# Attention scores of both maps from three products, the low part of the queries over 64 rows, in a two-layer hybrid mixer

## The chip, the cores and the metric

The kernel runs on one core of a Trainium2 chip. The metric is the device time of one execution in microseconds (us), the median of several runs. A page of one profiled execution and its trace were read as well.

## The reference, cut to what matters

Two layers are computed on 1024 latent tokens and 256 context tokens of width 1024. Only the attention matters here: 4 heads, two maps per head (m = 0, 1), 64 wide, over 1280 keys for a latent query.

```python
q_lat = apply_rope(rms_norm(split_heads_qk(q), qk_norm_g[0]), rope_cos, rope_sin)
k_lat = apply_rope(rms_norm(split_heads_qk(k), qk_norm_g[1]), rope_cos, rope_sin)
def diff_attend(q, k, v, lam):
    s = jnp.einsum('bhmqd,bhmkd->bhmqk', q, k).astype(jnp.float32) * (QK_DIM ** -0.5)
    p = jax.nn.softmax(s, axis=-1)
    p = p[:, :, 0] - lam * p[:, :, 1]
    return jnp.einsum('bhqk,bhkd->bhqd', p.astype(v.dtype), v)
```

## The kernel before, in words

The order of the work is written out by hand: every engine runs its instructions in the order in which the Python code calls them. PE is TensorE, DVE is VectorE, ACT is ScalarE, POOL is GpSimd and SP issues most DMAs.

Each layer first makes the gates, the Fourier and pooling parts and a first share of the output projection. Then come the projections of keys, queries and values (line 360, two token tiles of 128 per "post"), and then the attention. In a post of keys or queries (`qk_post`) DVE applies the rotary tables; for the keys the factor of the norm is multiplied on one post later (`k_late`), and for the queries it is kept aside in `rq` and enters only at the exponential. The unscaled queries are stored to memory (`qd`) and read back per tile.

For precision, each query and key is split into a high and a low part. The keys stand transposed in `kT`, one tensor per head and map, with the high part in rows 0 to 63 and the low part in rows 64 to 127. The query stands as [high, low] and [low, high], so that two matmuls over 128 rows give all four products.

The attention goes over units: one token tile of 128 queries and one head, 4 units to a tile, and in layer 0 two more units for the two context tiles. `step(i)` puts parts of four units side by side:

- unit i: the scores of map 0 and, later in the step, those of map 1 (line 915, six matmuls each), the row maxima (line 925) and their product with the norm factor (line 928) on DVE, the exponentials on ACT (line 943)
- unit i-1: `combine` joins the two maps (lines 952 to 969, DVE and POOL)
- unit i-2: `p_trans` transposes the probabilities in pieces of 4, 4 and 2 blocks (line 982, copied out by line 985 on DVE for the first piece and line 987 on ACT for the others), and `pv` multiplies with the values (line 998, copied out by line 1001 on ACT)
- unit i+1: `q_trans` transposes the split queries (line 894, copied out by line 901 on ACT); unit i+2: `q_split` on DVE

When a tile's four units are done, `z_trans` transposes its result (line 1031), ACT copies the high part out (line 1034) and DVE makes the low part (`z_low`, line 1039). In the same step follows the first half of the tile's output projection and in the next step the second half (line 1061, twelve matmuls each). `PIECES` and `ENDS` name these steps.

PSUM has 8 banks: two score tiles of three banks (`PS`), and two banks for everything else (`PX`). A matmul that starts a score tile waits until the exponential that read the same tile before is done.

On ACT, `pv`'s copy (line 1001) stands between the exponentials of the two maps:

```python
            if old:
                pv(old)
            if cur:
                expo(cur, 1)
```

Of the kernel before, what the change touches and what calls it, by code (L numbers as in the profile page):

```python
# [31 lines left out]
def build(tc, I, out):  # L32
# [52 lines left out]
    # silu(c) = 0.5 c (1 + tanh(c/2))  # L85
# [44 lines left out]
    def mod_finish(l, k, sh, scl):  # L130
        """sh, scl: [128, n, 2] products for the n channel tiles from k on"""
# [11 lines left out]
    def mod0_load(q):  # L143
        """shift and scale for the channel tiles 2q and 2q + 1"""
# [46 lines left out]
    def mod_acc(src, c0, sides, res, eng2=None):  # L191
        """elementwise over k: acc[p, s, col] = sum_k w[k*128+p, col] * silu(c)_s[k*128+p] for 512 columns"""
# [66 lines left out]
    def x_rms(x, r):  # L259
        """r = 1 / rms of the rows of x"""  # L260
# [90 lines left out]
    def proj_tok(H, W, npair, post):  # L351
        """token-major [128 tokens, 256 columns], two token tiles to a bank"""
# [42 lines left out]
    def fourier_fft(A, ntok):  # L395
        """8-point transform over the high digit of the token; 2-point for the context"""
# [90 lines left out]
    def pooling(l, ct, wpb, gs, b, ntok):  # L487
        psc = pscT[:, l, ct:ct + 1]
        zs = []
        for c0, L in ((0, SEQ), (SEQ, CTX)):  # L490
# [17 lines left out]
            else:  # L508
                # windows of 8 replace those of 2, and of 16 those of 4
# [22 lines left out]
    def layer(l, src, dst, carry):  # L532
# [19 lines left out]
        # ---- tokens, and with them the fourier gate  # L552
# [106 lines left out]
        # small tables for what follows  # L659
# [58 lines left out]
        # ---- rest of the output projection, its loads ahead of the stores of the gates  # L718
# [45 lines left out]
        # ---- k, q, v  # L764
# [69 lines left out]
        for c in range(2):  # L834
            W = w_get()
            proj_tok(H, W, npA, qk_post(0, c))
# [520 lines left out]
```

## Time and profile before

| | |
|---|---|
| median of 3 runs | 1475.15 us (1474.24 to 1475.6) |
| span of the profiled execution | 1476.5 us, the only time given for it, 1.35 us above the median |
| busy: PE, DVE, POOL, ACT | 1391.2, 992.0, 774.4, 579.9 us |
| attention, layer 0 and layer 1 | about 505 to 815 us and 1199 to 1476 us of the span |
| matmuls of the scores, line 915 | 768 with 184.4 us busy, besides those of the context tiles |
| row maxima, line 925; the products behind them, line 928 | 132 each; 194.9 us and 85.0 us busy |

Busy time counts the whole of each instruction, and matmuls overlap, so a busy PE need not be the limit. What a stage is worth is read from the wait that ends last in it.

### The profile page before, as it was taken

To read this page: it belongs to the slowest core of one execution; us is meant where nothing else is said; L and a number is where in the kernel's file an instruction comes from. 1 tells how busy PE (TensorE), PEld (TensorE's weight loads), DVE (VectorE), ACT (ScalarE), POOL (GpSimd) and SP (SyncE) were. 2 spreads that over 40 slices of the span, in tenths; PEclk is the share of its full clock that TensorE was granted. 3 is DMA by queue.
4 is the path that set the end of the run, shared out by engine and by line. 5 is a ranking of instruction groups with operands and counts; after the bars stand their busy time and mean duration, and the time that the engine had idled before them with its cause. 6 is when DMAs were issued, how large, how long until landed. Compare 5 with 4: busy or idle time off the path is not lost.

```text
span 1476.5 us, 24260 instructions
## 1 busy us (share of the span) xinstructions
PE 1391.2 (94%) x9364; PEld 1245.2 (84%) x9364; DVE 992.0 (67%) x1667; ACT 579.9 (39%) x1230; POOL 774.4 (52%) x827
## 2 busy tenths in 40 slices
PE   7899999899999988899998999999999998999998
PEld 1678899789999977888887788888999997888887
DVE  2854458876883298788988653482564249888995
ACT  2633112101323274666665342120232236565663
POOL 2543122557783066666667742245986027666663
PEclk9999999999999999999999999999999999999999
DMA  9221332673232121112113222527212111111210
GB/s 353 96 85 33 127 112 90 223 247 126 72 115 72 57 73 58 58 46 70 44 66 107 83 64 81 177 82 243 99 55 93 45 44 44 43 44 44 77 39 30
DMA packets 65155, 137.09 MB, mean 93 GB/s; under 512 B 7312, under 2 KB 19728, under 8 KB 65040
## 3 DMA queue, kind: packets, MB, share of 16 engines
q1 hardware_dynamic: 49712, 108.82, 22.1%
q10 hardware_dynamic: 15328, 26.72, 5.3%
q8 instruction: 74, 1.21, 0.4%
q14 instruction: 41, 0.34, 0.1%
HBM read 105.63 MB, written 29.88 MB: 92 GB/s over the span
## 4 chain that ended last, share of the span: by engine, by line
PE 48%; DVE 22%; issue 4%; POOL 3%; DMA 3%; ACT 2%; ACTq 0%; POOLq 0%; DVEq 0%; SPq 0%
PE x L360 18%; DVE sm L925 7%; PE x L1061 6%; PE S L915 6%; PE x L340 5%; PE x L998 5%; DVE sm L928 3%; PE x L753 3%; PE x L982 2%; DVE t L985 1%; DVE qs L882 1%; DMA xpart<-e 1%; DVE t L210 1%; PE x L894 1%; PE x L856 1%
## 5 line engine op out<-in xcount | busy, mean ns | idle before, releaser
L360 PE MATMUL x<-wh,t 128*128 128x256 f32 x2432 | 445.0, 284 | 0.0
L360 PEld LDWEIGHTS x<-wh,t 128*128 128x128 f32 x2432 | 380.7, 192 | 1.8 <-issue 1.0
L360 PE MATMUL x<-wl,t 128*128 128x256 f32 x1216 | 344.3, 283 | 1.4 <-DVE wl L318 0.9
L925 DVE TENSOR_REDUCE sm<-S 128x1 f32<-128x1280 f32 (+1 forms) x132 | 194.9, 1477 | 73.6 <-PE S L915 72.6
L360 PEld LDWEIGHTS x<-wl,t 128*128 128x128 f32 x1216 | 233.0, 192 | 3.1 <-issue 1.2
L943 ACT ACTIVATE t<-S,sm,rq 128x1280 f32<-128x1280 f32 (+1 forms) x140 | 184.5, 1321 | 24.4 <-DVE sm L928 23.4
L915 PE MATMUL S<-t,e 128*128 128x512 f32 (+1 forms) x768 | 184.4, 376 | 3.0 <-ACT e L901 1.5
L340 PE MATMUL x<-t,wh 128*128 128x512 f32 (+1 forms) x640 | 172.0, 379 | 10.1 <-DVE t L289 5.1
L998 PE MATMUL x<-t,t 128*128 128x128 f32 x1312 | 159.1, 277 | 2.3 <-DVE t L985 1.7
L998 PEld LDWEIGHTS x<-t,t 128*128 128x128 f32 x1312 | 155.6, 194 | 5.5 <-DVE t L985 2.0
L915 PEld LDWEIGHTS S<-t,e 128*128 128x128 f32 x768 | 128.7, 193 | 21.9 <-ACT t L943 2.8
L340 PEld LDWEIGHTS x<-t,wh 128*128 128x128 f32 x640 | 113.2, 190 | 33.1 <-DVE t L289 5.9
L318 POOL TENSOR_TENSOR wl<-st,wh 128x1024 fp32r<-128x1024 f32 x36 | 92.7, 2576 | 86.3 <-ACT wh L317 85.7
L317 ACT ACTIVATE wh<-st 128x1024 fp32r<-128x1024 f32 x64 | 64.8, 1058 | 138.8 <-DMA xpart<-e 45.0
L966 POOL TENSOR_TENSOR t<-t,t 128x768 f32<-128x768 f32 (+1 forms) x64 | 116.1, 1813 | 5.3
L958 POOL TENSOR_SCALAR t<-t,sm 128x768 f32<-128x768 f32 x62 | 85.6, 1381 | 51.9 <-DVE sm L954 33.2
L982 PE MATMUL x<-ident,t 128*128 128x128 f32 x636 | 102.6, 277 | 6.0 <-DVE e L1064 4.9
L1061 PE MATMUL x<-wh,e 128*128 128x512 f32 (+1 forms) x312 | 100.3, 389 | 3.9 <-ACT t L987 2.7
L753 PE MATMUL x<-wh,t 128*128 128x512 f32 x288 | 93.5, 403 | 8.9 <-DVE t L528 4.7
L340 PE MATMUL x<-t,wl 128*128 128x512 f32 (+1 forms) x320 | 99.5, 372 | 0.0
L210 DVE SCALAR_TENSOR_TENSOR t<-t,sc,t 128x512 f32<-128x512 f32 x98 | 92.2, 982 | 2.2 <-DMA t<-in_wmB_dram 1.8
L982 PEld LDWEIGHTS x<-ident,t 128*128 128x128 f32 x636 | 75.1, 142 | 17.1 <-DVE e L1064 7.5
(225 smaller groups left out, 2324.6 us busy)
## 6 DMA issues: line engine op xcount, KB each, us to landing
st<-in_w_in_dram SPq DMA_DIRECT2D x48, 512.0 KB, 4.2
t<-in_wmB_dram ACTq DMA_DIRECT2D x24, 512.0 KB, 5.4
xpart<-e ACTq DMA_DIRECT2D x36, 256.0 KB, 4.4
t<-xpart SPq DMA_DIRECT2D x18, 512.0 KB, 3.9
t<-in_wmS_dram SPq DMA_DIRECT2D x16, 512.0 KB, 9.4
st<-in_w_out_dram SPq DMA_DIRECT2D x16, 512.0 KB, 4.7
t<-in_x_dram SPq DMA_DIRECT2D x10, 512.0 KB, 10.3
e<-in_x_dram SPq DMA_DIRECT2D x20, 256.0 KB, 4.8
```

The lines of the kernel that those rows point to most:

```text
L210: dve.scalar_tensor_tensor(a, w, sk, a, MULT, ADD)
L318: lo_eng[hf].tensor_tensor(lo[:, sl, :], st, hi[:, sl, :].bitcast(F32), SUB)
L340: pe.matmul(p[:, :m], lhsT=W[wi][:, k, ct * 128:ct * 128 + 128], rhs=H[k][hi][:, c0:c0 + m], start=(n == 0), stop=(n == 3 * KT - 1))
L360: pe.matmul(bank[:, i * 256:i * 256 + 256], lhsT=H[k][hi][:, j * 128:j * 128 + 128], rhs=W[wi][:, k, :], start=(n == 0), stop=(n == 3 * KT ...
L753: pe.matmul(ps, lhsT=zr[k][zi][:, j * 128:j * 128 + 128], rhs=W[wi][:, k, :], start=(n == 0), stop=(n == 11))
L915: pe.matmul(S[:, i * nk + c:i * nk + c + n], lhsT=s["qT"][i][:, m * 2 + f, :], rhs=kT[2 * h + m][:, k0 + c:k0 + c + n], start=(f == 0), st ...
L925: dve.tensor_reduce(mx, S[:, :nh * nk].rearrange("p (h k) -> p h k", h=nh), AX.X, ALU.max)
L943: act.activation(p[:, sl], S[:, sl], AF.Exp, bias=nb[:, i:i + 1], scale=rqs[:, i:i + 1], accum_out=ls[:, i:i + 1])
L966: pool.tensor_tensor(p[0][:, cut:end], p[0][:, cut:end], p[1][:, cut:end], ADD)
L982: pe.transpose(ps[:, i * 128:i * 128 + 128], s["p"][0][:, (t0 + i) * 128:(t0 + i + 1) * 128], ident)
L998: pe.matmul(o[:, i * 128:i * 128 + 128], lhsT=s["PT"][:, i * nkt + t, :], rhs=vv[h][:, kt0 + t, :], start=(t == 0), stop=(t == nkt - 1))
L1061: pe.matmul(ps[:, :m], lhsT=zz[:, k, :], rhs=Wa[hf][wi][:, k, w0:w0 + m], start=(n == 0), stop=(n == 11))
```

## The change

The queries get the norm factor before they are stored: it is multiplied with -0.125 and applied one post later by the same function that did so for the keys (`qk_late`). So the scores come out negated and scaled, the row minimum is already the bias of the exponential, and `rq` and the small product of line 928 are gone.

The scores take three products. The query stands as [high, high] over 128 rows, which with the keys gives high times high and high times low, and as the low part alone, over 64 rows: rows 0 to 63 for map 0 and rows 64 to 127 for map 1. For the latter the keys of odd maps stand as [low, high]. Both maps of a unit are now computed in one call: three matmuls of map 0 and three of map 1 over 128 rows, and then six over 64 rows, alternately of map 0 and map 1. `combine` stands ahead of the scores, and both row minima follow them.

```diff
-        def k_late():
+        def qk_late():
             if late:
-                p, c, t1, ss = late.pop()
+                qk, p, c, t1, ss = late.pop()
                 t3 = t1.rearrange("p t m e -> p (t m) e")
                 dve.tensor_tensor(t3, t3, ss.unsqueeze(2).to_broadcast([128, 8, 64]), MULT)
+                if qk == 0:
+                    for i in range(2):
+                        sp.dma_start(qd[l][2 * p + i, :, c * 256:c * 256 + 256], t1[:, i].rearrange("p m e -> p (m e)"))
+                    return
                 for m in range(4):
...
                 if qk == 0:
-                    pool.tensor_scalar(rq[:, 2 * p:2 * p + 2, 4 * c:4 * c + 4],
-                                       ss.rearrange("p (a b) -> p a b", b=4), 0.125, 0.0, MULT, ADD)
+                    pool.tensor_scalar(ss, ss, -0.125, 0.0, MULT, ADD)
...
-                if qk == 0:
-                    for i in range(2):
-                        sp.dma_start(qd[l][2 * p + i, :, c * 256:c * 256 + 256], t1[:, i].rearrange("p m e -> p (m e)"))
-                else:
-                    k_late()
-                    late.append((p, c, t1, ss))
+                qk_late()
+                late.append((qk, p, c, t1, ss))
...
-        def score(u, m):
+        def score(u):
             s = st[u]
             k0, nk = rng(u)
-            S = PS()
+            S = [PS(), PS()]
+            def mm(i, h, m, f, c):
+                n = min(512, nk - c)
+                r = slice(64 * m, 64 * m + 64) if f else slice(0, 128)
+                pe.matmul(S[m][:, i * nk + c:i * nk + c + n], lhsT=s["qT"][i][r, m * 2 + f, :],
+                          rhs=kT[2 * h + m][r, k0 + c:k0 + c + n], start=(f == 0), stop=(f == 1))
             for i, h in enumerate(heads(u)):
-                for f in range(2):
+                for m in range(2):
                     for c in range(0, nk, 512):
-                        n = min(512, nk - c)
-                        pe.matmul(S[:, i * nk + c:i * nk + c + n], lhsT=s["qT"][i][:, m * 2 + f, :],
-                                  rhs=kT[2 * h + m][:, k0 + c:k0 + c + n], start=(f == 0), stop=(f == 1))
+                        mm(i, h, m, 0, c)
+                for c in range(0, nk, 512):
+                    for m in range(2):
+                        mm(i, h, m, 1, c)
...
-            mx = SM(nh)
-            dve.tensor_reduce(mx, S[:, :nh * nk].rearrange("p (h k) -> p h k", h=nh), AX.X, ALU.max)
             nb = SM(nh)
-            dve.scalar_tensor_tensor(nb, mx, -1.0, rqs, MULT, MULT)
+            dve.tensor_reduce(nb, S[:, :nh * nk].rearrange("p (h k) -> p h k", h=nh), AX.X, ALU.min)
...
             if old:
                 p_trans(old, 0)
+            if prev and i > 1:
+                combine(prev)
             if cur:
-                score(cur, 0)
+                score(cur)
             if old:
                 p_trans(old, 4)
+            if cur:
+                row_max(cur, 0)
             if 2 in fin:
                 z_trans(fin[2])
             if 2 in fin and 0 <= i - 3 < N:
                 sub_norm(units[i - 3])
             if cur:
-                row_max(cur, 0)
+                row_max(cur, 1)
             if 2 in fin:
                 z_low(fin[2])
...
             if nxt:
                 q_trans(nxt)
-            if prev and i > 1:
-                combine(prev)
-            if cur:
-                score(cur, 1)
-            if cur:
-                row_max(cur, 1)
             if old:
                 p_trans(old, 8)
```

Three places show the order. On PE, in a step of layer 1 before the change, from the scores of map 0 on (`S_` is a score tile, the operands are keys `t_` and transposed queries `e_`; L982 is `p_trans`, L894 `q_trans`):

```order
L915 MATMUL S_14659<-t_1984_11835,e_2641_14597 128x512 [waits Activation_49]
L915 MATMUL S_14659<-t_1984_11835,e_2641_14597 128x512
L915 MATMUL S_14659<-t_1984_11835,e_2641_14597 128x256
L915 MATMUL S_14659<-t_1984_11835,e_2641_14597 128x512 x2
L915 MATMUL S_14659<-t_1984_11835,e_2641_14597 128x256
L982 MATMUL x_14666<-ident,t_2623_14524 128x128 [waits Activation_49,Pool_49]
L982 MATMUL x_14666<-ident,t_2623_14524 128x128 x3
L894 MATMUL x_14676<-identR,qs_14625 128x128 [waits DVE_49]
L894 MATMUL x_14676<-identR,qs_14625 128x128 x3
L915 MATMUL S_14693<-t_1991_11911,e_2641_14597 128x512 [waits Activation_49]
L915 MATMUL S_14693<-t_1991_11911,e_2641_14597 128x512
L915 MATMUL S_14693<-t_1991_11911,e_2641_14597 128x256
```

And on PE in such a step now, from the first score matmul to the last:

```order
L917 MATMUL S_13784<-t_1925_11808,e_2358_13738 128x512 [waits Activation_49]
L917 MATMUL S_13784<-t_1925_11808,e_2358_13738 128x512
L917 MATMUL S_13784<-t_1925_11808,e_2358_13738 128x256
L917 MATMUL S_13785<-t_1930_11876,e_2358_13738 128x512 [waits Activation_49]
L917 MATMUL S_13785<-t_1930_11876,e_2358_13738 128x512
L917 MATMUL S_13785<-t_1930_11876,e_2358_13738 128x256
L917 MATMUL S_13784<-t_1925_11808,e_2358_13738 128x512
L917 MATMUL S_13785<-t_1930_11876,e_2358_13738 128x512
L917 MATMUL S_13784<-t_1925_11808,e_2358_13738 128x512
L917 MATMUL S_13785<-t_1930_11876,e_2358_13738 128x512
L917 MATMUL S_13784<-t_1925_11808,e_2358_13738 128x256
L917 MATMUL S_13785<-t_1930_11876,e_2358_13738 128x256
```

The first matmul on the second map's tile, which waits for ACT, stood behind a piece of `p_trans` and behind `q_trans`; now it is the fourth score matmul, and those two stand behind all scores.

On ACT before, from the exponential of map 0 on (L943 exponential, L1001 copy of `pv`, L987 copy of `p_trans`):

```order
L943 ACTIVATE t_2419_13756,sm_13757<-S_13702,sm_13717,rq_10361 128x1280 [waits DVE_49,Pool_49]
L1001 ACTIVATE t_2367_13561<-x_13776 128x128 [waits PE_49]
L943 ACTIVATE t_2424_13788,sm_13789<-S_13736,sm_13745,rq_10361 128x1280 [waits DVE_49]
L1009 ACTIVATE t_2367_13561,sm_13791<-t_2367_13561 128x128 [waits Activation_49,Pool_49]
L987 ACTIVATE t_2428_13796<-x_13810 128x512 [waits PE_49]
```

And on ACT now (L949, L1007, L1015 and L993 are the same four lines):

```order
L949 ACTIVATE t_2315_13568,sm_13569<-S_13528,sm_13548 128x1280 [waits DVE_49,Pool_49]
L1007 ACTIVATE t_2267_13381<-x_13588 128x128 [waits PE_49]
L949 ACTIVATE t_2320_13600,sm_13601<-S_13529,sm_13550 128x1280 [waits DVE_49]
L1015 ACTIVATE t_2267_13381,sm_13603<-t_2267_13381 128x128 [waits Activation_49,Pool_49]
L993 ACTIVATE t_2324_13608<-x_13639 128x512 [waits PE_49]
```

Nothing moved here: the exponential of map 1 still stands behind the copy of `pv`.

On DVE before, at the head of a step with `z_trans` (L985 copy of `p_trans`, L925 row maximum of map 0, L1039 `z_low`, L952 to L957 `combine`):

```order
L985 COPY t_2474_13963<-x_13964 128x512 [waits PE_49]
L925 TENSOR_REDUCE sm_13996<-S_13970 128x1 [waits PE_49]
L928 SCALAR_TENSOR_TENSOR sm_13998<-sm_13996,rq_10361 128x1 [waits DVE_49]
L1039 TENSOR_TENSOR e_2480_13989<-x_13983,e_2479_13988 128x512 [waits Activation_49]
L952 RECIPROCAL sm_14008<-sm_13961 128x1
L954 SCALAR_TENSOR_TENSOR sm_14010<-sm_13946,lamneg_102,sm_14008 128x1 [waits DVE_49]
L957 SCALAR_TENSOR_TENSOR t_2469_13945<-t_2472_13960,sm_14010,t_2469_13945 128x512 [waits DVE_49]
```

And on DVE now (L991 is the copy, L958 to L963 `combine`, L934 the row minima, L1045 `z_low`):

```order
L991 COPY t_2366_13767<-x_13768 128x512 [waits PE_49]
L958 RECIPROCAL sm_13774<-sm_13765 128x1 [waits Activation_49]
L960 SCALAR_TENSOR_TENSOR sm_13776<-sm_13750,lamneg_102,sm_13774 128x1 [waits DVE_49]
L963 SCALAR_TENSOR_TENSOR t_2361_13749<-t_2364_13764,sm_13776,t_2361_13749 128x512 [waits DVE_49]
L934 TENSOR_REDUCE sm_13804<-S_13784 128x1 [waits PE_49]
L934 TENSOR_REDUCE sm_13819<-S_13785 128x1 [waits PE_49]
L1045 TENSOR_TENSOR e_2377_13812<-x_13806,e_2376_13811 128x512 [waits Activation_49]
```

`z_low` stood behind one row maximum and ahead of `combine`; now it stands behind `combine` and both row minima.

## Rows read from the trace of the kernel before

**Rows 1.** Stretch of layer 1's attention: us; busy PE, PEld, DVE, ACT, POOL; clock; DMA

```profile
1320.00:1360.00 40.00, 38.74 (x267) 34.58 (x266) 35.32 (x65) 23.76 (x50) 25.00 (x33) 1.00 0.12 41
```

**Rows 2.** Groups by line: xcount, busy us, mean ns, idle before

```profile
L925 DVE TENSOR_REDUCE sm<-S 128x1 f32<-128x1280 f32 (+1 forms) x132 | 194.9, 1477 | 73.6 <-PE S L915 72.6 <-ACT t L943 1.1
...
L928 DVE SCALAR_TENSOR_TENSOR sm<-sm,rq 128x1 f32<-128x1 f32 (+1 forms) x132 | 85.0, 644 | 4.9
...
L787 DVE TENSOR_TENSOR e<-e,sm 128x512 f32<-128x512 f32 x20 | 15.6, 782 | 5.2 <-POOL e L815 5.2
...
L1039 DVE TENSOR_TENSOR e<-x,e 128x512 fp32r<-128x512 f32 x18 | 12.4, 687 | 2.0 <-ACT e L1034 1.8
```

**Rows 3.** Timeline of a step without output projection: start us, duration us, engine, line

```profile
709.89 2.31 PEld L998 LDWEIGHTS x<-t,t 128*128 128x128 f32 x20
709.99 2.40 PE L998 MATMUL x<-t,t 128*128 128x128 f32 x20
...
712.23 0.60 PE L982 MATMUL x<-ident,t 128*128 128x128 f32 x4
712.26 1.28 DVE L928 SCALAR_TENSOR_TENSOR sm<-sm,rq 128x1 f32<-128x1 f32 x1
712.49 0.27 ACT L1001 ACTIVATE t<-x 128x128 f32<-128x128 f32 x1
...
714.93 1.48 DVE L925 TENSOR_REDUCE sm<-S 128x1 f32<-128x1280 f32 x1
...
715.28 0.58 ACT L987 ACTIVATE t<-x 128x512 f32<-128x512 f32 x1
...
715.75 0.59 ACT L901 ACTIVATE e<-x 128x512 fp32r<-128x512 f32 x1
716.45 0.16 DVE L928 SCALAR_TENSOR_TENSOR sm<-sm,rq 128x1 f32<-128x1 f32 x1
...
716.89 2.40 PE L998 MATMUL x<-t,t 128*128 128x128 f32 x20
```

**Rows 4.** Timeline of DVE, map 0's row maxima of the next steps and `z_low`

```profile
721.82 1.48 DVE L925 TENSOR_REDUCE sm<-S 128x1 f32<-128x1280 f32 x1
723.41 0.68 DVE L1039 TENSOR_TENSOR e<-x,e 128x512 fp32r<-128x512 f32 x1
...
731.38 1.49 DVE L925 TENSOR_REDUCE sm<-S 128x1 f32<-128x1280 f32 x1 [0.55 <-PE S L915]
...
740.28 1.49 DVE L925 TENSOR_REDUCE sm<-S 128x1 f32<-128x1280 f32 x1 [0.48 <-PE S L915]
```

**Rows 5.** Chain that ended last: start us, us, engine and line, count

```profile
413.21 21.74 PE x L360 x179
...
1291.37 1.17 PE S L915 x6
1292.53 0.44 PE x L982 x4
...
1294.72 2.73 PE x L1061 x12
1297.45 2.23 PE x L998 x20
```

**Rows 6.** Timeline where a score matmul waited for an exponential

```profile
512.30 1.43 ACT L943 ACTIVATE t<-S,sm,rq 128x1280 f32<-128x1280 f32 x1
...
513.61 0.22 ACT L943 ACTIVATION_READ_ACCUMULATOR t<-S,sm,rq 128x1 f32 x1
...
513.88 0.50 PE L915 MATMUL S<-t,e 128*128 128x512 f32 x1 [0.67 <-ACT t L943]
```

**Rows 7.** The same view around idle stretches of PE (clock is the third last)

```profile
1235.00:1240.00 5.00, 3.46 (x27) 3.06 (x26) 4.93 (x6) 4.42 (x9) 4.74 (x5) 1.00 0.00 0
1240.00:1245.00 5.00, 3.75 (x16) 3.36 (x17) 4.47 (x8) 0.91 (x3) 2.95 (x5) 0.66 0.63 202
1255.00:1260.00 5.00, 3.19 (x24) 2.84 (x24) 4.08 (x6) 1.97 (x5) 4.14 (x4) 1.00 0.00 0
```

More of the change, by code (lines that the diff above doesn't have):

```diff
@@ L832, in layer @@
             proj_tok(H, W, 5, qk_post(1, c))
-        k_late()
         for c in range(2):
@@ L836, in layer @@
             proj_tok(H, W, npA, qk_post(0, c))
+        qk_late()
         st = {}
@@ L875, in q_split @@
                 if n == 1:
-                    qs = e2p.tile([128, 2, 192], F32R, tag="qs", name=nm("qs"), bufs=2)
+                    qs = e2p.tile([128, 1, 6, 64], F32R, tag="qs", name=nm("qs"), bufs=2)
                 else:
-                    qs = T5([128, 4, 192], F32R)
-                qv = st[u[0]]["q"][:, h * 128:h * 128 + n * 128].rearrange("p (m e) -> p m e", e=64)
-                dve.tensor_copy(qs[:, :, 0:64], qv)
-                dve.tensor_tensor(qs[:, :, 64:128], qv, qs[:, :, 0:64].bitcast(F32), SUB)
-                dve.tensor_copy(qs[:, :, 128:192], qs[:, :, 0:64].bitcast(F32))
-                s["qs"] += [qs[:, 2 * i:2 * i + 2, :] for i in range(n)]
+                    qs = T5([128, 2, 6, 64], F32R)
+                qv = st[u[0]]["q"][:, h * 128:h * 128 + n * 128].rearrange("p (n m e) -> p n m e", m=2, e=64)
+                dve.tensor_copy(qs[:, :, 1:5:3, :], qv)
+                dve.tensor_tensor(qs[:, :, 0:6:5, :], qv, qs[:, :, 1:5:3, :].bitcast(F32), SUB)
+                dve.tensor_copy(qs[:, :, 2:4, :], qs[:, :, 1:5:3, :].bitcast(F32))
+                s["qs"] += [qs[:, i].rearrange("p a e -> p (a e)") for i in range(n)]
         def q_trans(u, half=0):
@@ L890, in q_trans @@
                 ps = PX(F32R)
-                for m in range(2):
-                    for f in range(2):
-                        o = (m * 2 + f) * 128
-                        pe.transpose(ps[:, o:o + 128], qs[:, m, 64 * f:64 * f + 128], identR)
+                for o, a in enumerate((64, 0, 192, 256)):
+                    pe.transpose(ps[:, o * 128:o * 128 + 128], qs[:, a:a + 128], identR)
                 if one:
@@ L905, in rng @@
             return (SEQ, CTX) if u[0] >= 8 else (0, NTOK)
-        def score(u, m):
+        def score(u):
             s = st[u]
             k0, nk = rng(u)
-            S = PS()
+            S = [PS(), PS()]
[4 more added lines that the diff above has]
+                          rhs=kT[2 * h + m][r, k0 + c:k0 + c + n], start=(f == 0), stop=(f == 1))
             for i, h in enumerate(heads(u)):
-                for f in range(2):
+                for m in range(2):
                     for c in range(0, nk, 512):
-                        n = min(512, nk - c)
-                        pe.matmul(S[:, i * nk + c:i * nk + c + n], lhsT=s["qT"][i][:, m * 2 + f, :],
-                                  rhs=kT[2 * h + m][:, k0 + c:k0 + c + n], start=(f == 0), stop=(f == 1))
-            s["S%d" % m] = S
+                        mm(i, h, m, 0, c)
+                for c in range(0, nk, 512):
+                    for m in range(2):
+                        mm(i, h, m, 1, c)
+            s["SS"] = S
         def row_max(u, m):
@@ L922, in row_max @@
             nh = len(hs)
[L923 to L925 removed]
+            S = s["SS"][m]
             nb = SM(nh)
[L927 to L929 removed]
+            dve.tensor_reduce(nb, S[:, :nh * nk].rearrange("p (h k) -> p h k", h=nh), AX.X, ALU.min)
+            s["S"].append((S, nb))
         def expo(u, m):
@@ L933, in expo @@
             nk = rng(u)[1]
-            S, nb, rqs = s["S"][m]
+            S, nb = s["S"][m]
             if u == units[0]:
```

13 lines of the change are left out of this document (5 added, 8 removed).

## The prediction

> **What bounds the kernel now.** I looked first at the busy time by stretch. In the attention PE is busy for 38.7 of 40 us, at the full clock, and DVE for 35.3 [rows 1]. Both are close to full, so I went on to the timeline of single steps. The step between the row maxima at 714.93 and 721.82 has no output projection and takes 6.89 us [rows 3, 4]. The next one has `z_trans` and the first half of an output projection and takes 9.56 us, the one after it has the second half and takes 8.90 us [rows 4]. A tile is four such steps.
>
> In the plain step DVE is the limit. Its two row maxima take 1.48 us each and the product behind them 1.28 us in one place and 0.16 us in the other [rows 3]. In the steps with an output projection PE is, which issues twelve more matmuls in 2.73 us [rows 5]. What matters for the change is what is not a limit now: the exponential of map 1 starts only behind the copy of `pv`, yet nobody waits for it, because the scores of map 1 come late in the step.
>
> **What the change removes.** Line 928 goes, 132 instructions and 85.0 us of DVE [rows 2], 1.44 us in a plain step. PE's six score matmuls take 1.17 us per map [rows 5], 2.34 us for both. The six products over 128 rows that stay take half of it, 0.59 us per map. The trace has no matmul over 64 rows. If the two of a pair run side by side, the three pairs take at least 0.59 us; one after the other they take 1.17 us. Each still loads its own weights, and twenty loads of `pv` take 2.31 us [rows 3], which makes 0.69 us for six. I take 0.70 us, near the low end, because the loads would then set the pace, and keep both ends.
>
> The Trainium skill bears on this in "TensorE: Matmul & The Clock Gate", Part 3: matmuls whose operands sit in different row groups run at the same time, and a pack takes about the time of one matmul. No row here shows it. By this rule the pairs take 0.59 us and the sum below would be 6 us lower.
>
> **What it adds ahead of the attention.** A DVE multiplication per post of the queries, 18 of them at 0.78 us like those of the keys [rows 2], 14 us in all. They lie beside the projections, where PE runs 179 matmuls in 21.74 us without a gap, 5.8 us for the 48 of a post [rows 5]. Uncovered they would cost the 14 us. The stores of the queries go out one post later on SP's queue, and the first read of them stands behind the last; five posts of the values, 29 us, cover it. The last post of the keys is finished one post later too, and its readers, the transposes of the keys, stand beside the values. The other new forms (`q_split` with its parts in another order, the keys with halves swapped) have the same counts and sizes as before. All of this I put at zero.
>
> **What it moves: a plain step.** The scores now need both score tiles at once. I count from T, when PE has issued `pv` and begins the next step (712.23 before [rows 3]).
> - PE issues four transposes in 0.44 us [rows 5] and the first map's three scores by 1.03. The fourth score matmul needs the exponential of the unit before on map 1.
> - ACT starts the copy of `pv` at T + 0.26 for 0.27 us [rows 3]; the exponential follows at 0.55. It takes 1.53 us with the reading of its sum, and PE goes on 0.05 us behind it [rows 6], so at T + 2.13. PE has stood still for 1.10 us. Queued behind the waiting matmul are all later transposes, `q_trans` and `pv`, and DVE's row minima wait for them.
> - The rest of the scores: 0.59 + 0.70, until 3.42. Four transposes, until 3.86.
> - ACT copies them from 4.06 on (their record is 0.16 us longer than their issue, and some 0.04 us follow). The copy of `q_trans` behind it ends 1.06 us after that start (715.28 to 716.34 [rows 3]), at 5.12. `pv` takes the bank that this copy frees, so it starts at 5.17, and with 2.23 us [rows 5] ends at T + 7.40.
>
> The step is 7.40 us for 6.89, 0.51 longer, although DVE has 1.44 us less to do. The old limit has been replaced by a loop: copy of `pv`, exponential, scores, transposes, copies, `pv`.
>
> **Steps with an output projection.** In the step with the second half, the projection takes the place of `pv` at 5.17: 2.73 and 2.23 us more give 10.13 for 8.90, 1.23 longer. In the step with `z_trans` the projection takes the bank that `z_low` reads. `z_low` now stands behind both row minima. They can start 0.20 us behind the last score, at 3.62, take 1.51 us each with the gap, and end at 6.64; `z_low` takes 0.69 [rows 2], until 7.33. The projection starts at 7.38 and the step ends at 12.34 for 9.56, 2.78 longer.
>
> **The sum.** There are 66 units (132 row maxima), 34 in layer 0 and 32 in layer 1, and 18 `z_low` [rows 2]. By the order of the tiles two of these lie behind all scores, one is in a step without a first half, and two share a step with another tile's second half. So 15 steps get 2.78, 12 get 1.23. Of the other 35 steps from the third on I count 25 at 0.51, and the five at the head of each layer, which are uneven before too, at zero (5 us more if they too become 0.51 longer). That is 41.7 + 14.8 + 12.8 = 69.2 us. On the span of 1476.5 us it makes 1545.7 us. The span lies 1.35 us above the median of the runs, so I predict 1544 us. With the pairs at 0.59 us it is 1539 us.
>
> **Rivals.** *Pairs one after the other:* 0.47 us more in 52 steps, 24 us, 1569 us. The changed program gives them separate rows of the array, so I hold this for unlikely.
>
> *Switching between 128 and 64 rows empties PE.* If PE finishes everything in flight before the pairs and again behind them, each switch costs the tail of a matmul, 0.17 us (the record of `pv` is 2.40 us, its issue 2.23 [rows 3, 5]): 0.34 us in 52 steps, 18 us, 1562 us. No row here has such a switch in a busy stretch. The skill's "TensorEngine Tiling (Array Packing)", Key Properties, says that a change of the tiling mode drains the engine; it gives no price.
>
> *The clock falls.* After stretches with 3.46 us busy in 5, PE ran the next 5 us at 0.66 of the full clock, so 3.4 us of them at 1.2 GHz and not 2.4, which is 1.7 us of work lost; after one with 3.19 us it stayed up [rows 7]. The new step with `z_trans` has about 3.9 us issued in its first 7.4 us. If the clock falls in each of the 15, it costs 25 us: 1570 us.
>
> *`z_low` holds nobody up:* then that step is 10.13 us and the 0.44 us of its own transposes, 1.77 less in 15 steps, 1517 us. Against it stands the bank that the projection takes.
>
> *Faster.* If the exponential of map 1 ends by T + 1.03, PE never waits, and the freed DVE time counts. PE's own issue in a plain step is 2.23 for `pv`, 1.10 for ten transposes, 0.44 for `q_trans` and 1.87 for the scores, 5.64 us. That is 1.25 less in 25 steps, 0.53 in 12 (8.37 for 8.90) and 0.75 in 15 (8.81 for 9.56): 49 us less, 1426 us. It turns on the place of the copy of `pv` ahead of this exponential. Taken behind it, the exponential could run while `pv` does. The order rows say it is not moved. The same loop without its wait in the middle, by chance just as long as the old limits, would be no change.
>
> **Chances.** My forecast 0.52, with its own range 1530 to 1557; switching 0.13; clock 0.13; pairs in series 0.08; `z_low` harmless 0.06; faster 0.06; no change 0.02. The range 1520 to 1585 holds the first four, and the end lies above 1570 because the two costs of PE can come together. What can be told from no change is about 0.2%, 3 us: slower 0.92, same 0.02, faster 0.06.
>
> **What would show it.** In the trace after, the score matmuls should show idle time of PE ahead of them, released by the exponential, about 1 us in nearly every step; plain steps should be 7.4 us from one row minimum to the next of the same map; `z_low` should end more than 3 us later in its step than now, with PE idle ahead of the projection. DVE's share in the attention should fall well below 35 of 40 us. Six score matmuls over 64 rows in about 0.7 us would show that pairs run side by side, 1.2 us that they don't. I am wrong if the exponential of map 1 is found done when the fourth score matmul comes up, or if steps stay below 7 us.

## The result, and the profile after

The changed kernel takes 1555.64 us (median of 4 runs, 1549.33 to 1557.3), the kernel before in the same session 1475.38 us (4 runs, 1474.24 to 1478.85). The ratio is 1.0534, with a 95% interval of 1.0504 to 1.0564. The profiled execution has a span of 1555.5 us, 79.0 us more than before. The time lies in the predicted range, 12 us above the predicted 1544.

The page of the changed kernel first: busy time of PE, DVE and ACT, shares of the chain that ended last, and two groups of instructions with their idle time before.

```profile
PE 1416.3 (91%) x9364; PEld 1219.3 (78%) x9364; DVE 915.7 (59%) x1553; ACT 565.7 (36%) x1230; POOL 764.8 (49%) x827
...
PE 58%; ACT 11%; DVE 5%; issue 5%; POOL 2%; DMA 1%; ACTq 0%; POOLq 0%; DVEq 0%
...
L917 PE MATMUL S<-t,e 128*128 128x512 f32 (+3 forms) x768 | 158.5, 393 | 46.1 <-ACT t L949 44.7
...
L1067 PE MATMUL x<-wh,e 128*128 128x512 f32 (+1 forms) x312 | 103.9, 401 | 11.0 <-DVE e L1045 7.0
```

DVE has 76 us less to do than before (992.0 us), and ACT now carries a tenth of the chain. Line 917, the scores, let PE stand for 46.1 us, nearly all of it until the exponential of line 949. The output projection waits 7.0 us for `z_low` (line 1045).

The busy time by stretch (columns as in [rows 1]): 40 us of layer 1's attention, then two places of 5 us with the clock falling, one at the head of layer 0 and one inside layer 1.

```profile
1360.00:1400.00 40.00, 34.03 (x229) 27.05 (x227) 26.61 (x45) 21.07 (x45) 21.92 (x28) 1.00 0.16 55
...
515.00:520.00 5.00, 3.42 (x25) 2.71 (x24) 1.55 (x3) 3.31 (x6) 2.80 (x4) 1.00 0.77 243
520.00:525.00 5.00, 4.34 (x18) 3.05 (x17) 2.80 (x5) 1.07 (x4) 3.51 (x4) 0.52 0.45 177
...
1300.00:1305.00 5.00, 3.74 (x10) 2.83 (x11) 2.56 (x6) 3.25 (x7) 3.18 (x6) 0.68 0.00 0
```

PE is busy for 34.0 of 40 us where it was 38.7, and DVE for 26.6 where it was 35.3 [rows 1]. No engine is full any more: the step is a loop through several engines.

The timeline of a plain step shows that loop (columns as in [rows 3]; the bracket is the idle time ahead and what ended it).

```profile
1363.84 0.60 PE L988 MATMUL x<-ident,t 128*128 128x128 f32 x4
...
1364.04 0.28 ACT L1007 ACTIVATE t<-x 128x128 f32<-128x128 f32 x1 [0.86 <-PE x L1004]
...
1364.22 1.32 ACT L949 ACTIVATE t<-S,sm 128x1280 f32<-128x1280 f32 x1
...
1365.43 0.20 ACT L949 ACTIVATION_READ_ACCUMULATOR t<-S,sm 128x1 f32 x1
...
1365.68 1.62 PE L917 MATMUL S<-t,e 128*128 128x512 f32 x9 [0.65 <-ACT t L949]
...
1366.45 0.53 PEld L917 LDWEIGHTS S<-t,e 64*128 64x128 f32 x6 [0.24 <-issue]
1367.23 0.42 PEld L988 LDWEIGHTS x<-ident,t 128*128 128x128 f32 x4 [0.25 <-issue]
...
1368.42 0.59 ACT L901 ACTIVATE e<-x 128x512 fp32r<-128x512 f32 x1
...
1369.07 2.50 PE L1004 MATMUL x<-t,t 128*128 128x128 f32 x20
...
1371.40 0.60 PE L988 MATMUL x<-ident,t 128*128 128x128 f32 x4
```

PE begins the step with the transposes at 1363.84 and the next at 1371.40: 7.56 us. (The prediction counts from the same matmul record, 712.23 in [rows 3].) In between one reads the copy of `pv` (1007), the exponential behind it (949), the nine scores that wait for it, the copies, and `pv` again. The 64-row loads and the loads behind them each start after a gap of 0.24 to 0.25 us that nothing but the change of row count accompanies.

In the steps with an output projection, the row minima of DVE give the lengths, 12.17 us and 10.32 us, and `z_low` ends 0.05 us before the projection begins.

```profile
1374.91 2.89 DVE L934 TENSOR_REDUCE sm<-S 128x1 f32<-128x1280 f32 x2 [0.49 <-PE S L917]
...
1377.72 0.68 DVE L1045 TENSOR_TENSOR e<-x,e 128x512 fp32r<-128x512 f32 x1
...
1378.45 0.50 PE L1067 MATMUL x<-wh,e 128*128 128x512 f32 x1 [0.60 <-DVE e L1045]
...
1387.08 2.89 DVE L934 TENSOR_REDUCE sm<-S 128x1 f32<-128x1280 f32 x2 [0.48 <-PE S L917]
1397.40 2.89 DVE L934 TENSOR_REDUCE sm<-S 128x1 f32<-128x1280 f32 x2 [0.48 <-PE S L917]
```

### The profile page after: what moved, and what is told of

Same layout as the page of the kernel before. It is cut to its first block, busy times and chain, and to the rows that moved or that the text cites. A ratio compares the mean times of both kernels' runs of the same rounds, so it can differ in the third digit from the quotient of the medians.

```text
span 1555.5 us, 24024 instructions
## 1 busy us (share of the span) xinstructions
PE 1416.3 (91%) x9364; PEld 1219.3 (78%) x9364; DVE 915.7 (59%) x1553; ACT 565.7 (36%) x1230; POOL 764.8 (49%) x827
## 4 chain that ended last, share of the span: by engine, by line
PE 58%; ACT 11%; DVE 5%; issue 5%; POOL 2%; DMA 1%; ACTq 0%; POOLq 0%; DVEq 0%
PE x L360 23%; PE x L1004 9%; PE S L917 7%; PE x L1067 7%; ACT t L949 6%; PE x L340 4%; PE x L753 4%; PE x L988 2%; ACT t L993 2%; ACT e L901 1%; DVE sm L934 1%; DMA t<-in_wmB_dram 1%; POOL e L759 1%; PE x L856 1%; DVE e L1045 1%
## 5 line engine op out<-in xcount | busy, mean ns | idle before, releaser
L934 DVE TENSOR_REDUCE sm<-S 128x1 f32<-128x1280 f32 (+1 forms) x132 | 189.5, 1477 | 83.4 <-PE S L917 83.4
L917 PE MATMUL S<-t,e 128*128 128x512 f32 (+3 forms) x768 | 158.5, 393 | 46.1 <-ACT t L949 44.7
L949 ACT ACTIVATE t<-S,sm 128x1280 f32<-128x1280 f32 (+1 forms) x140 | 171.5, 1229 | 0.1
L1004 PE MATMUL x<-t,t 128*128 128x128 f32 x1312 | 163.4, 280 | 5.2 <-DVE t L991 1.7
L917 PEld LDWEIGHTS S<-t,e 128*128 128x128 f32 (+1 forms) x768 | 94.9, 190 | 91.0 <-ACT t L949 64.4
L988 PE MATMUL x<-ident,t 128*128 128x128 f32 x636 | 107.8, 285 | 28.7 <-ACT t L993 16.5
L993 ACT ACTIVATE t<-x 128x512 f32<-128x512 f32 (+1 forms) x130 | 63.6, 492 | 147.0 <-PE x L988 145.4
L1067 PE MATMUL x<-wh,e 128*128 128x512 f32 (+1 forms) x312 | 103.9, 401 | 11.0 <-DVE e L1045 7.0
L988 PEld LDWEIGHTS x<-ident,t 128*128 128x128 f32 x636 | 69.9, 142 | 53.2 <-ACT t L993 22.8
L991 DVE COPY t<-x 128x512 f32<-128x512 f32 x66 | 45.6, 691 | 94.4 <-PE x L988 94.4
```

The source lines that it names most:

```text
L917: pe.matmul(S[m][:, i * nk + c:i * nk + c + n], lhsT=s["qT"][i][r, m * 2 + f, :], rhs=kT[2 * h + m][r, k0 + c:k0 + c + n], start=(f == 0), ...
L934: dve.tensor_reduce(nb, S[:, :nh * nk].rearrange("p (h k) -> p h k", h=nh), AX.X, ALU.min)
L949: act.activation(p[:, sl], S[:, sl], AF.Exp, bias=nb[:, i:i + 1], scale=-1.0, accum_out=ls[:, i:i + 1])
L988: pe.transpose(ps[:, i * 128:i * 128 + 128], s["p"][0][:, (t0 + i) * 128:(t0 + i + 1) * 128], ident)
L993: act.activation(PT, ps[:, :n * 128], AF.Copy)
L1004: pe.matmul(o[:, i * 128:i * 128 + 128], lhsT=s["PT"][:, i * nkt + t, :], rhs=vv[h][:, kt0 + t, :], start=(t == 0), stop=(t == nkt - 1))
```

## The experiments

My theory after the result was: the loss is the wait of PE for the exponential of map 1, behind the copy of `pv`; a smaller part is `z_low`; the three products themselves save little. The rivals were the forms of the matmuls (64 rows in series, or the change between 128 and 64 rows) and the added work on the queries. Each kernel below was timed in three rounds against the kernel before. Edits are shown against the changed kernel unless said otherwise.

### The exponential of map 1 ahead of the copy of `pv`

```diff
-            if old:
-                pv(old)
             if cur:
                 expo(cur, 1)
+            if old:
+                pv(old)
```

> The changed kernel with one edit: the exponential of map 1 stands ahead of the copy of pv on ACT. Theory (loop through the copy of pv): the fourth score matmul no longer waits, a plain step goes from 7.56 to about 6.5 us, the two steps with an output projection lose about 1 us each, 52 steps together some 50 us: about 1505 us. Rival (asking for both score tiles at once is itself the limit, through row minima and exponentials on DVE and ACT): the wait stays, only its releaser's time shifts, 1545 us or more.

Measured: 1507.33 us, ratio to before 1.0209 (1.019 to 1.0228). The timeline of DVE in this kernel, three pairs of row minima, and the page's group of the scores:

```profile
1330.38 2.89 DVE L934 TENSOR_REDUCE sm<-S 128x1 f32<-128x1280 f32 x2
1337.02 2.89 DVE L934 TENSOR_REDUCE sm<-S 128x1 f32<-128x1280 f32 x2
1348.22 2.89 DVE L934 TENSOR_REDUCE sm<-S 128x1 f32<-128x1280 f32 x2
...
L917 PE MATMUL S<-t,e 128*128 128x512 f32 (+3 forms) x768 | 147.9, 387 | 12.0 <-ACT t L949 9.4
```

Two instructions on ACT change places, and 48 us are back. PE's idle time at the scores falls from 46.1 to 12.0 us and a plain step of layer 1 from 7.56 to 6.64 us (in layer 0 to some 7.04); the step with `z_trans` is 11.20 us. This is the largest part of the loss, and it is shown.

### `z_low` ahead of the second row minimum

```diff
-            if cur:
-                row_max(cur, 1)
             if 2 in fin:
                 z_low(fin[2])
+            if cur:
+                row_max(cur, 1)
```

> The changed kernel with one edit: z_low stands ahead of the second row minimum on DVE. Theory (the output projection waits for z_low): the step with z_trans goes from 12.17 to about 11.4 us, 15 of them, 12 us less: about 1543 us. Rival (that step's end is set by the loop through the copy of pv and ACT's copies alone): within 3 us of 1555 us.

Measured: 1539.66 us, ratio 1.0422 (1.0403 to 1.044). DVE in the step with `z_trans`, and the group of the output projection:

```profile
1326.27 1.49 DVE L934 TENSOR_REDUCE sm<-S 128x1 f32<-128x1280 f32 x1 [0.49 <-PE S L917]
1327.98 0.69 DVE L1045 TENSOR_TENSOR e<-x,e 128x512 fp32r<-128x512 f32 x1 [0.22 <-ACT e L1040]
...
1337.49 2.89 DVE L934 TENSOR_REDUCE sm<-S 128x1 f32<-128x1280 f32 x2 [0.47 <-PE S L917]
...
L1067 PE MATMUL x<-wh,e 128*128 128x512 f32 (+1 forms) x312 | 100.4, 390 | 4.1 <-ACT t L993 1.4 <-ACT e L901 1.0 <-ACT e L1040 0.7
```

The step is 11.22 us for 12.17, and the projection hardly waits for `z_low` any more: its longest waits are now for copies of ACT. 16 us are back, about 0.95 in each of 15 such steps.

### Both repairs together

> Both edits, the exponential of map 1 ahead of the copy of pv and z_low ahead of the second row minimum. Theory: the gains add up, about 1490 us, and PE has hardly any idle time ahead of the scores. Rival (both edits relieve the same wait): no better than the first alone, about 1505 us.

Measured: 1490.47 us, ratio 1.0093 (1.0071 to 1.0115). The two repairs add up: 48 and 16 us apart, 65 together. A tile of layer 1 takes 33.07 us, where the changed kernel has 37.6 and the kernel before 32.2. So the changed order without its two waits is still slower than before. Its stretch of layer 1, and the page's groups of the scores and of the transposes of `p_trans`:

```profile
1300.00:1340.00 40.00, 37.25 (x255) 30.67 (x255) 29.10 (x52) 22.73 (x50) 24.54 (x33) 1.00 0.12 40
...
L917 PE MATMUL S<-t,e 128*128 128x512 f32 (+3 forms) x768 | 147.9, 387 | 12.3 <-ACT t L949 9.7
...
L988 PE MATMUL x<-ident,t 128*128 128x128 f32 x636 | 106.6, 283 | 26.4 <-ACT t L993 16.6
```

DVE has 11 us of 40 to spare, PE 3. PE still stands 38.7 us ahead of these two groups, for copies and exponentials of ACT above all.

### The queries alone

The kernel before with the part of the change that is on the queries, and nothing else: normalised and negated ahead, row minima, no product behind them, a constant -1 as the scale of the exponential; four products per map in the order of before. Against the kernel before:

```diff
-            mx = SM(nh)
-            dve.tensor_reduce(mx, S[:, :nh * nk].rearrange("p (h k) -> p h k", h=nh), AX.X, ALU.max)
...
-            dve.scalar_tensor_tensor(nb, mx, -1.0, rqs, MULT, MULT)
+            dve.tensor_reduce(nb, S[:, :nh * nk].rearrange("p (h k) -> p h k", h=nh), AX.X, ALU.min)
...
-                act.activation(p[:, sl], S[:, sl], AF.Exp, bias=nb[:, i:i + 1], scale=rqs[:, i:i + 1], accum_out=ls[:, i:i + 1])
+                act.activation(p[:, sl], S[:, sl], AF.Exp, bias=nb[:, i:i + 1], scale=-1.0, accum_out=ls[:, i:i + 1])
...
```

> The kernel before with the query part of the change alone: queries negated and normalised ahead, row minima as bias, no small product on DVE; four products, maps one after the other, order of the steps as before. Theory (in plain steps DVE was the limit, of which 1.44 us go; the others were held by PE): plain steps fall from 6.89 to between 6.1 and 6.5 us, 25 to 32 of them: 1455 to 1465 us. Rival (the multiplication added to the queries or the stores one post later cost as much): 1475 us or more.

Measured: 1449.82 us, ratio 0.9802 (0.9786 to 0.9819): faster than both kernels. Its stretch of layer 1, two row minima of map 0 a plain step apart, and the same two groups (lines 916 and 980 here):

```profile
1300.00:1340.00 40.00, 39.44 (x272) 35.48 (x272) 35.42 (x55) 24.00 (x51) 26.25 (x34) 1.00 0.13 41
...
1343.06 1.49 DVE L926 TENSOR_REDUCE sm<-S 128x1 f32<-128x1280 f32 x1 [0.47 <-PE S L916]
...
1349.63 1.47 DVE L926 TENSOR_REDUCE sm<-S 128x1 f32<-128x1280 f32 x1
...
L916 PE MATMUL S<-t,e 128*128 128x512 f32 (+1 forms) x768 | 182.0, 373 | 2.8 <-ACT e L902 1.4
...
L980 PE MATMUL x<-ident,t 128*128 128x128 f32 x636 | 101.7, 275 | 5.7 <-DVE e L1062 4.1
```

The plain step is 6.57 us for 6.89 [rows 3, 4], and PE is busy for 39.4 of 40 us. It stands 8.5 us ahead of the scores and the transposes, 30 less than with three products and both repairs.

Why 0.32 us, when line 928 took 1.44 us of DVE in that step? DVE is as full as before, 35.4 of 40 us for 35.3 [rows 1], and over the whole execution its busy time falls by 12 us (992.0 to 979.9), not by the 85.0 of line 928. The next small instruction, the scaling of `pv`'s result, has taken the long one's place. Its group before and here, the addition of POOL that runs beside line 928 before, and the instruction in the step above:

```profile
L1025 DVE SCALAR_TENSOR_TENSOR e<-t,sm,e 128x128 f32<-128x128 f32 x62 | 23.2, 374 | 5.5 <-POOL sm L1017 5.5
```

```profile
L1023 DVE SCALAR_TENSOR_TENSOR e<-t,sm,e 128x128 f32<-128x128 f32 x62 | 83.1, 1341 | 5.7 <-POOL sm L1015 5.7
```

```profile
711.68 1.84 POOL L966 TENSOR_TENSOR t<-t,t 128x768 f32<-128x768 f32 x1
```

```profile
1346.98 1.52 DVE L1023 SCALAR_TENSOR_TENSOR e<-t,sm,e 128x128 f32<-128x128 f32 x1
```

Before, line 928 runs from 712.26 to 713.54 [rows 3] and POOL's addition in `combine` (line 966) ends at 713.52; all 55 records of line 928 over 1 us end within 0.02 us of such an addition. Here line 1023 ends at 1348.50, 0.15 us behind the same addition (line 964, 1346.52 to 1348.35), and so do 55 of its 59 records over 1 us. So some 1.1 of the 1.28 us was no work of line 928: the first small instruction behind the second row reduction is held until POOL's addition is over, whichever it is. Why DVE is held is not shown. Of the 1.44 us that left a plain step, 1.17 came back in line 1023, and 0.27 is close to the 0.32 gained.

The time is below what I expected, the plain step above it (6.1 to 6.5 us). The rest of the 29 us comes from the other steps: a tile of layer 1 takes 31.23 us for 32.2, and from the first score matmul to the first `z_low` it is 73.1 us for 80.3 in layer 0 and 72.1 for 78.0 in layer 1.

The added multiplications and the later stores cost little if anything. The first score matmul of layer 0 starts between 478.1 and 482.3 us in the eleven kernels that have them, and at 478.35 in the one trace of before. In layer 1 it starts 358.6 to 362.5 us behind the last `z_low` of layer 0, before 361.1.

### Three products in the order of before

The kernel of the last section with three products: the 64-row matmuls stand alone, behind the 128-row ones of the same map. Queries and keys lie as in the changed kernel (not shown). Against the kernel with the queries alone:

```diff
-                        pe.matmul(S[:, i * nk + c:i * nk + c + n], lhsT=s["qT"][i][:, m * 2 + f, :],
-                                  rhs=kT[2 * h + m][:, k0 + c:k0 + c + n], start=(f == 0), stop=(f == 1))
+                        pe.matmul(S[:, i * nk + c:i * nk + c + n], lhsT=s["qT"][i][r, m * 2 + f, :],
+                                  rhs=kT[2 * h + m][r, k0 + c:k0 + c + n], start=(f == 0), stop=(f == 1))
...
```

where `r` is rows 0 to 127 for the first part and the map's 64 rows for the second.

> The changed kernel's queries and its three products (low query over 64 rows), but map by map in the order of the steps of before, so that the low products of a map follow each other on the same rows. Theory (the loss is in asking for both maps at once): faster than the changed kernel by 40 us or more, about 1490 us, and slower than the version with the queries alone, by two switches per map of about 0.2 us each, 30 us or so. Rival (splitting the rows is what costs): no faster than the changed kernel, 1550 us.

Measured: 1489.18 us, ratio 1.0077 (1.0053 to 1.0101), 39 us above the kernel with four products. The weight loads of the 64-row products by shape, first of this kernel, then of the changed kernel:

```profile
L916 PEld LDWEIGHTS S<-t,e 64*128 64x128 f32 x384 | 62.3, 187 | 38.7 <-issue 32.5
```

```profile
L917 PEld LDWEIGHTS S<-t,e 64*128 64x128 f32 x384 | 31.9, 189 | 19.2 <-issue 16.3
```

The same 384 loads take 62.3 us here and 31.9 us where both maps are computed together. And this kernel changes the row count four times a step for two, with 32.5 us of gaps ahead of these loads for 16.3. So three products lose in this order too. Both maps in one call halve these two costs, but even with both repairs that kernel, at 1490.47 us, is no better than this one. It stands 38.7 us ahead of the scores and the transposes, as shown above, and this one 6.7 us; that these waits eat the saving fits the numbers, but no run takes them apart.

### All low products over 128 rows

```diff
-                r = slice(64 * m, 64 * m + 64) if f else slice(0, 128)
+                r = slice(0, 128)
```

The output then counts one of the products twice; the instructions and their order are those of the changed kernel, without any 64-row matmul.

> The changed kernel with the six low products over all 128 rows, so that the array is never split; the product of high query and low key is then counted twice, and the output is off by that. Theory (the six over 64 rows with two switches take about 1 us, six over 128 rows 1.17 us): about 0.2 us more in 62 steps, 13 us more: about 1568 us. Rival 1 (the switches cost as much as the pairs save): 1555 us. Rival 2 (the pairs save their full half): 36 us more, 1591 us.

Measured: 1568.98 us, ratio 1.0612 (1.0592 to 1.0631). The loads of the nine score matmuls behind the exponential are now one run without a gap:

```profile
1340.94 1.81 PEld L917 LDWEIGHTS S<-t,e 128*128 128x128 f32 x9 [0.98 <-ACT t L949]
```

The transposes behind them start 1.75 us after the first of the nine, in the changed kernel 1.55 us after (1365.68 to 1367.23). So the 64 rows save 0.20 us a step, with their two gaps paid, and 13 us in all, as expected.

### The six low products map by map, and in the same rows

Two kernels ask what makes the six 64-row products cheap. The first takes three of map 0 and then three of map 1, and no longer alternates:

```diff
-                for c in range(0, nk, 512):
-                    for m in range(2):
+                for m in range(2):
+                    for c in range(0, nk, 512):
                         mm(i, h, m, 1, c)
```

> The changed kernel with the six matmuls over 64 rows in another order: three of map 0, then three of map 1, so that neighbours use the same rows. Theory (pairs over different rows run side by side): the scores take about 0.5 us more in each of 62 steps, 30 us more: about 1585 us. Rival (they never ran side by side, the gain in PE time came from elsewhere): within 3 us of 1555 us.

Measured: 1554.98 us, ratio 1.0526 (1.0506 to 1.0546): no change, and my expectation was wrong. The second keeps the alternation and puts the low parts of both maps in rows 0 to 63 (queries and keys are laid out to match, not shown):

```diff
-                r = slice(64 * m, 64 * m + 64) if f else slice(0, 128)
+                r = slice(0, 64) if f else slice(0, 128)
...
```

> The changed kernel, with the low parts of both maps in the same rows 0 to 63 instead of half of the rows each; number, size and order of the nine matmuls are unchanged, so the result differs only in which rows the six 64-row products use. Theory (the 64-row products of the two maps are cheap because they lie in different rows and run side by side): the six now take about .5 us more in each of 62 steps, about +30 us, some 1587 us. Rival (it is the alternation of tiles, or the small row count by itself, that makes them cheap): as the changed kernel, 1555 us.

Measured: 1598.81 us, ratio 1.0808 (1.0785 to 1.083). The six loads in the first and in the second kernel, and two row minima of the second:

```profile
1346.65 0.54 PEld L917 LDWEIGHTS S<-t,e 64*128 64x128 f32 x6 [0.25 <-issue]
```

```profile
1350.31 1.22 PEld L917 LDWEIGHTS S<-t,e 64*128 64x128 f32 x6 [0.25 <-issue]
...
1359.79 2.89 DVE L934 TENSOR_REDUCE sm<-S 128x1 f32<-128x1280 f32 x2 [0.94 <-PE S L917]
1367.93 2.89 DVE L934 TENSOR_REDUCE sm<-S 128x1 f32<-128x1280 f32 x2 [0.94 <-PE S L917]
```

What counts is that the two maps lie in different rows: 0.54 us for six loads, whatever their order, and 1.22 us in the same rows. The Trainium skill states this in "TensorE: Matmul & The Clock Gate", Part 3: matmuls in different row groups run at the same time. The traces agree, and show that they need not alternate for it: in the first kernel the six start in pairs all the same, 512 columns at 1346.65 and 1346.66 and again at 1346.99 and 1347.01, and 256 columns at 1347.22 and 1347.23, though the program has all three of map 0 first.

In the second kernel the plain step grows to 8.14 us, 0.58 more, which is 36 us over 62 steps. The other 7 us fit the clock: in layer 1 four of six steps with `z_trans` take 14.2 us at a granted clock of 0.88, and two 12.6 us at full clock; in the changed kernel one of six is hit.

### Six changes of row count

```diff
-                for m in range(2):
-                    for c in range(0, nk, 512):
-                        mm(i, h, m, 0, c)
                 for c in range(0, nk, 512):
-                    for m in range(2):
-                        mm(i, h, m, 1, c)
+                    for f in range(2):
+                        for m in range(2):
+                            mm(i, h, m, f, c)
```

> The changed kernel with the nine products ordered by 512 columns: the 128-row products of a chunk, then its 64-row products, and so for the next chunk, so that TensorE changes between 128-row and 64-row products six times a step instead of two. Map 1's exponential is then waited for about .4 us earlier, which alone would cost some .39 us in 62 steps, about 1579 us. Theory (each change of row count costs .22 to .25 us of standing): .9 us a step more beside that, about 1630 us. Rival (a change costs nothing by itself, the idle .24 us is the end of the matmul before): about 1579 us.

Measured: 1647.28 us, ratio 1.1147 (1.1121 to 1.1173). Some of PE's weight loads in one step, the last row with two loads over 128 and two over 64 rows, and two row minima a plain step apart (the other lines stand two lower in this kernel):

```profile
1338.42 0.19 PEld L917 LDWEIGHTS S<-t,e 64*128 64x128 f32 x2 [0.36 <-issue]
1338.85 0.62 PEld L917 LDWEIGHTS S<-t,e 128*128 128x128 f32 x4 [0.24 <-issue]
...
1331.00 2.89 DVE L932 TENSOR_REDUCE sm<-S 128x1 f32<-128x1280 f32 x2 [1.09 <-PE S L917]
1339.70 2.89 DVE L932 TENSOR_REDUCE sm<-S 128x1 f32<-128x1280 f32 x2 [1.09 <-PE S L917]
```

There is a gap at each of the six changes, in both directions: 0.24, 0.25, 0.36 and 0.24 us at the first four, 0.14 and 0.13 at the last two. The time grows by 92 us. The plain step at full clock takes 8.70 us for 7.56, 1.14 more. The earlier wait for the exponential would make about 0.39 of it, an estimate, and the four changes that were added 0.75, some 0.19 us each. Over 62 steps that is 71 us. The other 21 fit the clock: its mean over the execution is 0.964 here and 0.978 in the changed kernel, which makes 59 and 34 us of full-clock work lost. "TensorEngine Tiling (Array Packing)" of the Trainium skill says in Key Properties that a change of the tiling mode drains TensorE; the gaps agree with it.

### One more wait removed

On top of both repairs, the transposes of the tile before are placed ahead of the scores, so that ACT's copy of them (line 993) runs while PE makes the scores:

```diff
+            if old:
+                p_trans(old, 4)
             if cur:
                 score(cur)
-            if old:
-                p_trans(old, 4)
```

> Both repairs (exponential of map 1 ahead of the copy of pv, z_low ahead of the second row minimum) and one more: the transposes of the combined probabilities of the tile before stand ahead of the score products, so that ScalarE's copy of them runs while TensorE makes the scores. With the two repairs TensorE still stood about .4 us a step waiting for that copy. Theory (that wait is on the path in most steps): .2 to .4 us in about 50 steps, 1470 to 1480 us for 1490 us. Rival (the wait moves to the row minima or to the exponential of the next tile): 1485 to 1495 us, no gain.

Measured: 1504.84 us, ratio 1.018 (1.016 to 1.02): 14 us slower than with the two repairs alone, and beyond both of my expectations. The attempt failed. PE in a plain step:

```profile
1325.09 0.63 PE L988 MATMUL x<-ident,t 128*128 128x128 f32 x4 [0.65 <-ACT t L1007]
...
1328.82 0.38 PE L1004 MATMUL x<-t,t 128*128 128x128 f32 x1 [0.44 <-ACT e L901]
```

The transposes now need the second of the two shared banks right behind `pv`, and `pv`'s result in it is copied out only behind both exponentials, from 1324.68 on. The scores had covered that copy. Later `pv` waits 0.44 us for the copy of `q_trans`. The wait for line 993, 16.6 us with the two repairs alone, gave way to these two, 1.09 us a step where it was 0.39, and the plain step at 1320.38 takes 7.32 us for 6.65.

## Why the prediction was right, point by point

**The wait for the exponential: right.** PE stops ahead of the fourth score matmul in 64 steps, released by line 949, and removing the wait alone gives back 48 us. It resumes 1.84 us after the step's start, not 2.13: the copy of `pv` starts at 0.20 us for 0.26 and the exponential at 0.38 for 0.55, and with its read it takes 1.41 us where I took 1.53 from before.

**The nine matmuls behind it: too cheap.** I priced them at 1.29 us, they take 1.55. The six 64-row ones do run side by side (0.53 us of loads for a predicted 0.70), so the rival of pairs in series is out; but the two gaps around them add 0.49. The rival that put a price on switching was right that there is one, at 0.34 a step for a measured 0.49; my sum had it at nothing.

**The plain step: 7.56 us for a predicted 7.40.** The two errors above, 0.29 us too long and 0.26 too short, cancel at the end of the scores (the transposes behind them start at 3.39 us for a predicted 3.42). That is luck. What is left comes behind it: the second `pv` starts at 5.23 us for 5.17 and takes 2.33 for 2.23.

**The steps with a projection: right in kind.** `z_low` ends 7.00 us into its step for a predicted 7.33, and the projection follows it; 12.17 and 10.32 us for 12.34 and 10.13. Moving `z_low` ahead of the second row minimum returns 16 us. One sign did not come: `z_low` was to end more than 3 us later in its step than before, and ends 2.04 later (before 724.09 in a step from 719.13, so at 4.96). The predicted 7.33 would not have given 3 either. A tile takes 37.6 us in the regular part, 37.27 by the prediction.

**The early steps: mis-sized.** I set the ten steps at the heads of the layers to zero. The first `z_low` of layer 0 starts at 571.81 us for 558.64 in the trace of before, 13.2 us later; the first of layer 1 at 1300.96 for 1250.26, of which 47.0 come from layer 0, so 3.7 us more. That is 17 us, more than the whole difference of 10 between the sum, 69.2, and the 79.0 measured. Of the 13.2 us, 4.0 lie ahead of the first score matmul (482.33 us for 478.35), which is scatter for the most part: in the ten other kernels with the same queries it starts between 478.1 and 481.9. The other 9.2 are the head itself, 89.5 us from there to `z_low` for 80.3. With both repairs the head takes 83.0 us. With all low products over 128 rows it takes 85.3 us, though each step is a little longer, and there the clock stays at 1.00 all through it. So the two waits make about half of the 9.2, an estimate, and the clock the rest.

**The rest** came out 7 us under the sum, which hides part of the 17, by luck again. It is not in the regular tiles (5.4 us longer each, 5.03 by the prediction), and I did not take the other steps apart. Between the first and the last `z_low` of each layer the time grows by 33.8 and 28.1 us, and by 0.3 behind. The last gap of layer 1 even falls, from 20.6 to 16.6 us, as no scores are left to wait for.

**The clock: a small part.** PE's granted clock was 0.52 from 520 to 525 us, so at 1.2 GHz for nearly all of it, after 5 us with 3.42 busy at 2.4 GHz. A few later steps with `z_trans` are hit too; the one that begins at 1298.16 takes 13.71 us, 1.54 more than the one at full clock, with a clock of 0.68 between 1300 and 1305. I had priced the rival at 15 such steps; 4 of those that the trace lets one measure are hit, and 3 before. Over the whole execution the mean clock is 0.978 of 1555.5 us for 0.985 of 1476.5, which is 34 and 22 us of full-clock work lost. So the clock makes at most 12 of the 79 us, and 7 of these 12 lie ahead of the attention.

**Queries and stores: right at zero.** The experiment on the queries alone is 2% faster than before. The prediction's account of what DVE's saved time is worth behind the new loop, nothing, held. But it took the 1.28 us of line 928 for work of DVE, and some 1.1 of them were a wait beside POOL. In the changed kernel that wait is gone, since the row minima now run beside POOL's addition and the scaling takes 374 ns as before (62 of line 1031, 23.2 us); in the old order it only moves to the next instruction.

The change is then three things: the query part, worth about -29 us; three products with both maps in one call, about +41 us even without the two waits (1490.47 for 1449.82); and the two waits of the new order, +65 us.

## What to carry to other kernels

A change that asks for two double-buffered tiles at once can turn slack between the engines into a wait: look for what the second tile's last reader is queued behind, and move that first. Packing matmuls over half the rows has a price at each end: here six in different rows saved 0.69 us of loads, and their two changes of row count cost 0.49. A small instruction with a long record may be waiting for another engine, and removing it can pass the wait on to the next. And time the parts of a change apart: here one part was a gain of 2% under a loss of 5%.

## What the runs showed of the hardware

A change between 128-row and 64-row matmuls stops the weight loads for 0.13 to 0.36 us in either direction. Six 64-row matmuls of 512 or 256 columns in two different halves of the rows load in 0.53 us, in the same half in 1.22 us; in different halves both orders that were run take the same. So two packed halves with their two changes take 1.02 us (1366.21 to 1367.23), where six full-row matmuls take 0.20 more.

The exponential of 128x1280 takes 1417 ns on average with the scale read per row and 1325 ns with a constant, in 124 instructions each, by the groups of line 943 before and 949 after:

```profile
L943 ACT ACTIVATE t<-S,sm,rq 128x1280 f32<-128x1280 f32 x124 | 175.7, 1417 | 24.4 <-DVE sm L928 23.4 <-POOL sm L968 1.1
```

```profile
L949 ACT ACTIVATE t<-S,sm 128x1280 f32<-128x1280 f32 x124 | 164.2, 1325 | 0.1
```

I had not priced this. "ScalarE: Activation LUTs" of the Trainium skill, in "What ACT_TABLE_LOAD costs", gives some 93 ns for each operand read per partition; the 92 ns here agree.

A DVE instruction whose operands all lie in SBUF, started while POOL adds 128x768 elements in `combine`, ends about when that addition does: 57 of line 928 take 1.27 us for 0.16 elsewhere, 54 of line 1023 1.52 us for 0.35. Those that read PSUM are not held: 58 row minima of the changed kernel start beside the addition and take 1.48 us, 16 `z_low` of the kernel with both repairs 0.69 us, both as elsewhere.
